# Row normalisation: loads and stores on two DMA queues, whole 8 MB tiles, rows split between VectorE and ScalarE

## The chip, the cores and the metric

The kernel runs on one core of a Trainium2 chip. The metric is the device time of one execution in microseconds (us), lower is better. Unless a sentence says otherwise, a time is the median of all timed runs of a kernel, and a ratio is the mean time of one kernel's fast runs over the mean time of the other's fast runs of the same rounds. So a ratio is not quite the ratio of the medians that are quoted.

"Span" is the profiled length.

## The reference

```python
def reference(x):                      # x: float32 [32, 512, 1024]
    sums = np.sum(np.abs(x), axis=-1, keepdims=True)
    return (x / (sums + 1e-8)).astype(np.float32)
```

There are 16,384 rows of 1,024 numbers. Every row is read once (67.11 MB in all), divided by the sum of its absolute values, and written once (67.11 MB).

## The kernel before

A tile is 128 partitions by 16 rows, 8 MB, so that each partition reads and writes 64 KB in one contiguous piece. There are eight tiles and three buffers. All transfers, loads and stores, go to one hardware queue, which is issued by SyncE. VectorE sums all 16 rows of a tile in one instruction and scales ten of them; ScalarE scales six. The last two tiles are handled in four chunks of four rows, and each chunk is stored as soon as it is ready.

```python
    def process_chunk(x_tile, out_ap, r0, rN, mv):
        ...
        nc.vector.tensor_reduce(out=s, in_=x_tile[:, r0 : r0 + rN, :], axis=X, op=add,
                                apply_absolute_value=True)
        nc.vector.reciprocal(out=inv, in_=s)
        for r in range(rN):
            if r < mv:  nc.vector.tensor_scalar_mul(...)      # row r of the chunk
            else:       nc.scalar.activation(..., func=Copy, scale=inv[:, r : r + 1])
        nc.sync.dma_start(out=out_ap[:, r0 : r0 + rN, :], in_=x_tile[:, r0 : r0 + rN, :])

    for i in range(ntiles):                                   # ntiles = 8, R = 16, MV = 10
        x_tile = sbuf.tile([P, R, d], x.dtype)                # BUFS = 3
        nc.sync.dma_start(out=x_tile[:, :, :], in_=x_t[i, :, :, :])
        if i < ntiles - 2:
            process_chunk(x_tile, out_t[i], 0, R, MV)
        else:
            C = 4
            for c0 in range(0, R, C):
                process_chunk(x_tile, out_t[i], c0, C, (MV * C) // R)
```

(Cut and shortened.) A scheduler orders these instructions. On the one queue it makes three loads, three stores, three loads, three stores, two loads, and then the eight chunk stores.

## Time and profile before

The time is 318.40 us (318.33 to 318.67, five runs). The next lines are from the page of the profiled execution: the span; the mean busy share of the 16 DMA engines in 40 slices of the span, in tenths; the DMA queue with its packets, MB and share of the 16 engines' time; the chain of waits by engine; and the three costliest groups (line, engine, operation, shapes, count | busy us, mean ns of one | idle time before them and its releaser).

```profile
span 316.9 us, 261 instructions
...
DMA  9999999999999999999999999999999999999797
...
q1 hardware_dynamic: 3168, 134.22, 98.6%
...
DVE 57%; DMA 35%; issue 4%; ACT 0%; ACTq 0%; SPq 0%; DVEq 0%
...
L37 DVE TENSOR_REDUCE s<-x_tile 128x4 f32<-128x4096 f32 (+1 forms) x14 | 138.3, 9891 | 111.2 <-DMA x_tile<-in_x_dram 111.2
L54 ACT ACTIVATE x_tile<-x_tile,inv 128x1024 f32<-128x1024 f32 x52 | 55.4, 1137 | 223.9 <-DVE inv L45 223.9
L48 DVE TENSOR_SCALAR x_tile<-x_tile,inv 128x1024 f32<-128x1024 f32 x76 | 51.4, 748 | 0.3
```

The queue line is the one that counts: one queue keeps 16 engines busy for 98.6% of the span. The chain of waits gives VectorE 57%, but that is the share of one dependency path. While VectorE works on a tile, the queue moves others. VectorE itself waits 111.2 us for loads.

In the records of single DMA packets, a packet of 64 KB takes 2.418 us at the median, and 16 engines x 65,536 B / 2.418 us is 433.7 GB/s. The Trainium skill, "DMA: Bandwidth & Descriptors", section "Where 436 GB/s comes from", puts the ceiling of the 16 ports at 435.2 GB/s; the trace agrees within 0.4%. One tile is 8 such packets on each engine, 19.35 us, and eight loads and eight stores are 309.5 us. A change can win only by taking idle time away from the DMA engines. For each kernel two numbers are therefore worked out from the packet records:

- *busy*: the summed durations of the data packets, divided by 16;
- *idle*: from the first data packet to the last, the time in which engines had no data packet, as a mean over the 16.

For the kernel before, busy is 312.3 us and idle is 2.1 us. The other 2.5 us of the span are before the first packet and after the last, less about 0.6 us in which two packets overlap on an engine and are counted twice.

### The profile page before, as it was taken

Reading aid. Unit: us, or ns where it says so; the run is one execution under the profiler, and the core shown is the slowest. Engines: PE = TensorE matmul, PEld = TensorE weight load, DVE = VectorE, ACT = ScalarE, POOL = GpSimd, SP = SyncE. Lnnn points to the kernel's source line nnn. Section 1 sums busy time; section 2 is a strip of 40 time slices with the busy share of each in tenths; the row PEclk is TensorE's granted clock in tenths of the full one; section 3 lists DMA queues with packets and bytes.
Section 4 is the critical chain, followed back from the end, with each engine's and each line's share of the span. In section 5 each row is a group of like instructions: output and inputs, shape, how many; then the busy total and the mean of one; then the engine's idle time right before and its main releaser. Section 6 shows DMA issues by size and latency. Waiting matters only on the chain.

```text
span 316.9 us, 261 instructions
## 1 busy us (share of the span) xinstructions
DVE 190.8 (60%) x104; ACT 56.7 (18%) x53; POOL 0.2 (0%) x4
## 2 busy tenths in 40 slices
DVE  0019999999990000039999999980000069999910
ACT  0010080080080000000160070080000002522520
POOL 0000000000000000000000000000000000000000
DMA  9999999999999999999999999999999999999797
GB/s 397 397 397 513 414 397 397 397 438 488 397 397 505 422 397 397 521 405 397 480 447 397 397 489 438 397 430 480 414 397 480 438 405 422 399 431 432 335 430 331
DMA packets 3170, 134.24 MB, mean 424 GB/s; under 512 B 352, under 2 KB 352, under 8 KB 352
## 3 DMA queue, kind: packets, MB, share of 16 engines
q1 hardware_dynamic: 3168, 134.22, 98.6%
q14 instruction: 2, 0.02, 0.0%
HBM read 67.11 MB, written 67.11 MB: 424 GB/s over the span
## 4 chain that ended last, share of the span: by engine, by line
DVE 57%; DMA 35%; issue 4%; ACT 0%; ACTq 0%; SPq 0%; DVEq 0%
DVE s L37 41%; DMA x_tile<-in_x_dram 35%; DVE x_tile L48 15%; DVE inv L45 1%; ACT x_tile L54 0%; ACTq L99 0%; SPq L60 0%; DVEq L45 0%; DVEq L48 0%
## 5 line engine op out<-in xcount | busy, mean ns | idle before, releaser
L37 DVE TENSOR_REDUCE s<-x_tile 128x4 f32<-128x4096 f32 (+1 forms) x14 | 138.3, 9891 | 111.2 <-DMA x_tile<-in_x_dram 111.2
L54 ACT ACTIVATE x_tile<-x_tile,inv 128x1024 f32<-128x1024 f32 x52 | 55.4, 1137 | 223.9 <-DVE inv L45 223.9
L48 DVE TENSOR_SCALAR x_tile<-x_tile,inv 128x1024 f32<-128x1024 f32 x76 | 51.4, 748 | 0.3
L54 ACT ACT_TABLE_LOAD x1 | 1.3, 1283 | 22.8 <-DMA x_tile<-in_x_dram 22.8
L45 DVE RECIPROCAL inv<-s 128x4 f32<-128x4 f32 (+1 forms) x14 | 2.6, 200 | 0.4
L88 POOL MEMSET const-bfloat16-1.0<- 128x1 bf16 x1 | 0.1, 101 | 0.0
L88 POOL MEMSET const-uint8-127<- 128x1 uint8 x1 | 0.1, 101 | 0.0
L88 POOL MEMSET const-float32-0.0<- 128x1 f32 x1 | 0.1, 98 | 0.2 <-issue 0.2
L88 POOL MEMSET const-float32-1.0<- 128x1 f32 x1 | 0.1, 98 | 0.0
## 6 DMA issues: line engine op xcount, KB each, us to landing
out_dram<-x_tile SPq DMA_DIRECT2D x8, 2048.0 KB, 9.9
x_tile<-in_x_dram SPq DMA_DIRECT2D x8, 51.0
out_dram<-x_tile SPq DMA_DIRECT2D x6, 29.5
```

The costliest lines, as they stand in the source:

```text
L37: nc.vector.tensor_reduce(out=s[:, :], in_=x_tile[:, r0 : r0 + rN, :], axis=mybir.AxisListType.X, op=mybir.AluOpType.add, apply_absolute_v ...
L45: nc.vector.reciprocal(out=inv[:, :], in_=s[:, :])
L48: nc.vector.tensor_scalar_mul(out=x_tile[:, r0 + r, :], in0=x_tile[:, r0 + r, :], scalar1=inv[:, r : r + 1],)
L54: nc.scalar.activation(out=x_tile[:, r0 + r, :], in_=x_tile[:, r0 + r, :], func=mybir.ActivationFunctionType.Copy, scale=inv[:, r : r + 1],)
L88: nc = _bacc.Bacc("TRN2", target_bir_lowering=False, num_devices=1)
```

## The change

The intent: two queues, so that stores do not line up behind loads; VectorE relieved by giving ScalarE seven rows to sum (absolute value with an accumulated sum, the result itself dropped into PSUM) and to scale; and simple whole-tile stores. Instructions stay in program order.

```diff
-    for i in range(ntiles):
-        x_tile = sbuf.tile([P, R, d], x.dtype)
-        nc.sync.dma_start(out=x_tile[:, :, :], in_=x_t[i, :, :, :])
-        if i < ntiles - 2:
-            process_chunk(x_tile, out_t[i], 0, R, MV)
-        else:
-            ...                                  # four chunks, four stores
+    DVE_PARTS = [(0, 5), (5, 9)]
+    ACT_PARTS = [(9, 13), (13, 16)]
+
+    def compute(x_tile):
+        sums = []
+        for a, b in ACT_PARTS:
+            s = stats.tile([P, b - a], FP32)
+            for r in range(a, b):
+                junk = psum.tile([P, d], FP32)
+                nc.scalar.activation(out=junk[:, :], in_=x_tile[:, r, :],
+                                     func=ACTF.Abs, accum_out=s[:, r - a : r - a + 1])
+            sums.append(s)
+        for k, (a, b) in enumerate(DVE_PARTS):
+            ...                                  # VectorE: reduce rows a..b, add EPS, reciprocal, scale
+            a2, b2 = ACT_PARTS[k]
+            inv2 = inverse(sums[k], b2 - a2)     # VectorE: add EPS, reciprocal
+            for r in range(a2, b2):
+                ...                              # ScalarE: scale row r by inv2 (Copy)
+
+    with tc.manual_schedule():
+        for i in range(ntiles):
+            x_tile = sbuf.tile([P, R, d], FP32)
+            nc.sync.dma_start(out=x_tile[:, :, :], in_=x_t[i])
+            compute(x_tile)
+            nc.gpsimd.dma_start(out=out_t[i], in_=x_tile[:, :, :])
```

(Shortened.) Below, tiles are counted from one: the last tile is the eighth, and "the seventh store" is the store of the seventh tile.

More of the change, by code (lines that the diff above doesn't have):

```diff
@@ L7 @@
 from concourse._compat import with_exitstack
+FP32 = mybir.dt.float32
+EPS = 1e-8
 @with_exitstack
@@ L18 @@
     P = nc.NUM_PARTITIONS
+    ACTF = mybir.ActivationFunctionType
     x_flat = x.flatten_outer_dims()
@@ L26 @@
     ntiles = n // (P * R)
+    BUFS = 3
     x_t = x_flat.rearrange("(n p r) d -> n p r d", p=P, r=R)
     out_t = out_flat.rearrange("(n p r) d -> n p r d", p=P, r=R)
-    BUFS = 3
     sbuf = ctx.enter_context(tc.tile_pool(name="sbuf", bufs=BUFS))
-    stats = ctx.enter_context(tc.tile_pool(name="stats", bufs=BUFS))
-    def process_chunk(x_tile, out_ap, r0, rN, mv):
-        s = stats.tile([P, rN], mybir.dt.float32, tag="s")
-        nc.vector.tensor_reduce(
-            out=s[:, :],
-            in_=x_tile[:, r0 : r0 + rN, :],
-            axis=mybir.AxisListType.X,
-            op=mybir.AluOpType.add,
-            apply_absolute_value=True,
-        )
-        inv = stats.tile([P, rN], mybir.dt.float32, tag="inv")
-        nc.vector.reciprocal(out=inv[:, :], in_=s[:, :])
-        for r in range(rN):
-            if r < mv:
+    stats = ctx.enter_context(tc.tile_pool(name="stats", bufs=6))
@@ new lines, with inverse @@
+    psum = ctx.enter_context(
+        tc.tile_pool(name="psum", bufs=2, space=bass.MemoryType.PSUM)
+    )
+    def inverse(s, k):
+        nc.vector.tensor_scalar_add(out=s[:, :], in0=s[:, :], scalar1=EPS)
+        inv = stats.tile([P, k], FP32)
+        nc.vector.reciprocal(out=inv[:, :], in_=s[:, :])
+        return inv
+    DVE_PARTS = [(0, 5), (5, 9)]
[6 more added lines that the diff above has]
+                junk = psum.tile([P, d], FP32)
+                nc.scalar.activation(
+                    out=junk[:, :],
+                    in_=x_tile[:, r, :],
+                    func=ACTF.Abs,
+                    accum_out=s[:, r - a : r - a + 1],
+                )
+            sums.append(s)
+        for k, (a, b) in enumerate(DVE_PARTS):
+            s = stats.tile([P, b - a], FP32)
+            nc.vector.tensor_reduce(
+                out=s[:, :],
+                in_=x_tile[:, a:b, :],
+                axis=mybir.AxisListType.X,
+                op=mybir.AluOpType.add,
+                apply_absolute_value=True,
+            )
+            inv = inverse(s, b - a)
+            for r in range(a, b):
+                row = x_tile[:, r, :]
@@ L48, in process_chunk @@
                 nc.vector.tensor_scalar_mul(
-                    out=x_tile[:, r0 + r, :],
-                    in0=x_tile[:, r0 + r, :],
-                    scalar1=inv[:, r : r + 1],
-                )
-            else:
+                    out=row, in0=row, scalar1=inv[:, r - a : r - a + 1]
+                )
+            a2, b2 = ACT_PARTS[k]
+            inv2 = inverse(sums[k], b2 - a2)
+            for r in range(a2, b2):
+                row = x_tile[:, r, :]
                 nc.scalar.activation(
-                    out=x_tile[:, r0 + r, :],
-                    in_=x_tile[:, r0 + r, :],
-                    func=mybir.ActivationFunctionType.Copy,
-                    scale=inv[:, r : r + 1],
-                )
@@ L60, in process_chunk @@
-        nc.sync.dma_start(out=out_ap[:, r0 : r0 + rN, :], in_=x_tile[:, r0 : r0 + rN, :])
-    MV = 10
-    for i in range(ntiles):
-        x_tile = sbuf.tile([P, R, d], x.dtype)
-        nc.sync.dma_start(out=x_tile[:, :, :], in_=x_t[i, :, :, :])
-        if i < ntiles - 2:
-            process_chunk(x_tile, out_t[i], 0, R, MV)
-        else:
-            C = 4
-            for c0 in range(0, R, C):
-                process_chunk(x_tile, out_t[i], c0, C, (MV * C) // R)
+                    out=row,
@@ L77 @@
+                    in_=row,
+                    func=ACTF.Copy,
+                    scale=inv2[:, r - a2 : r - a2 + 1],
+                )
+    with tc.manual_schedule():
[4 more added lines that the diff above has]
+            nc.gpsimd.dma_start(out=out_t[i], in_=x_tile[:, :, :])
 _INS = ['x']
```

## The prediction

> **What bounds the kernel now.** The DMA engines. Section 3 of the page: the one hardware queue takes 98.6% of the time of 16 engines, for 134.22 MB; section 2 shows DMA at nine tenths in nearly every slice. In the DMA records a 64 KB packet takes 2.418 us at the median, loads and stores alike: 16 x 65,536 B / 2.418 us = 433.7 GB/s. The Trainium skill, "DMA: Bandwidth & Descriptors", section "Where 436 GB/s comes from", gives 435.2 GB/s as the ceiling of the 16 ports; the trace agrees within 0.4%. One 8 MB tile is 8 packets per engine, 19.35 us; 16 tile transfers are 309.5 us of the 316.9 us span. The other 7 us are 2.7 before the first packet, 0.7 in slow first packets, small losses, and about 2 at the end. The chain of waits names VectorE for 57%; that misleads: while VectorE works, the queue moves other tiles.
>
> **What the change does.**
> - VectorE per tile falls from 17.2 (reduce of 16 rows) + 0.25 + 6.7 (ten scales) = 24.2 us to about 5.4 + 4.4 (reduces of 5 and 4 rows at 1.076 us) + 6.1 (nine scales at 0.67) + 1.2 for eight tiny instructions = 17 us.
> - ScalarE gets seven Abs passes with an accumulated sum (estimate 1.06 us each as the Copy has, plus 0.2 for the accumulator: 8.8 us) beside seven Copies (7.4 us). Its last three Copies wait for VectorE's last reciprocal, so a tile takes about 20.4 us from landing to store, against 24.2.
> - Neither is on the critical path in the middle: a tile's load and store take 38.7 us of DMA.
> - Loads and stores share the 16 engines from two queues; the bytes stay. A packet should look about twice as long while both are active, the total staying at about 430 GB/s.
> - The last two tiles are no longer stored in pieces. The last tile's compute (20.4 us, plus about 1.5 of software issue) hides behind the seventh store (19.35 us), except that the last load ends behind the sixth store (estimate 2 to 3 us, it was issued that much later). I expect 2 to 6 us of idle DMA there.
>
> The Trainium skill, "SBUF — State Buffer", section "SBUF: two separate sides", says that VectorE in a two-port mode locks GpSimd out of writing descriptors. The scales seem to run so (1024 elements in 0.67 us), but each of the eight stores is issued as VectorE starts a reduce; no run here shows it yet. I expect under 2 us.
>
> **Sum.** Head 2.7 + 0.7, transfers 309.5, gap 4, receipt and end 2: span about 319, and the timed runs read 1.45 us more: **320.0 us**, 0.5% slower, range 315.5 to 328. Chances: faster by over 2% 0.05, within 2% 0.75, slower by over 2% 0.20.
>
> **What the profile would show.** DMA queues together 96 to 98% of 16 engines' span, half each; VectorE busy about 136 us, ScalarE about 130; VectorE's idle time larger, released by load DMAs; the last store landing 20 to 21 us after its issue with nothing else moving, and a dip in DMA before it.
>
> **What would make it wrong.** Slower: packets of the software queue costing more than 2.418 us (smaller descriptors, ring fetches, writes and reads alternating): 3% on all would be 9 us; a late start of each software store; arbitration that makes the last tile late. Faster: two queues letting an engine overlap reads and writes beyond 434 GB/s, which nothing in the trace suggests.

## The result, and the profile after

The time is 326.98 us (325.81 to 329.18, five runs) against 318.40; the ratio is 1.0282, 95% interval 1.0252 to 1.0311. The change is 2.8% slower. Its runs also differ by 3.4 us, where those of the kernel before differ by 0.3.

The same lines of the page, for the changed kernel:

```profile
span 327.4 us, 415 instructions
...
DVE 137.3 (42%) x152; ACT 120.2 (37%) x169; POOL 4.6 (1%) x12
...
DMA  9899899899899998998999999999899998960695
...
q1 hardware_dynamic: 1152, 67.11, 48.0%
q0 software_dynamic: 1152, 67.11, 47.4%
...
L66 DVE TENSOR_REDUCE s<-x_tile 128x5 f32<-128x5120 f32 (+1 forms) x16 | 79.0, 4939 | 161.7 <-DMA x_tile<-in_x_dram 161.7
L57 ACT ACTIVATE junk<-x_tile 128x1024 f32<-128x1024 f32 x56 | 56.5, 1008 | 138.2 <-DMA x_tile<-in_x_dram 138.2
L83 ACT ACTIVATE x_tile<-x_tile,inv 128x1024 f32<-128x1024 f32 x56 | 59.9, 1137 | 45.6 <-DVE inv L44 45.6
```

VectorE went from 190.8 to 137.3 us and waits longer for loads, so it is not the limit. The queues together fell from 98.6% to 95.4% of the span, and the DMA row shows where: a hole in the 37th slice, near the end. The view of windows for the changed kernel gives it numbers (stretch in us: its length, busy time of VectorE, ScalarE and GpSimd with instruction counts, TensorE clock, DMA share, GB/s):

```profile
0.00:255.00 255.00, 114.56 (x125) 99.86 (x143) 3.53 (x10) 1.00 1.00 429
255.00:285.00 30.00, 6.50 (x10) 6.37 (x7) 0.53 (x1) 1.00 1.00 433
285.00:293.00 8.00, 7.90 (x8) 6.45 (x14) 0.00 (x0) 1.00 0.91 393
293.00:306.00 13.00, 8.32 (x12) 7.49 (x7) 0.53 (x1) 1.00 0.05 20
306.00:328.00 22.00, 0.00 (x0) 0.00 (x0) 0.00 (x0) 1.00 0.88 381
```

The kernel before, same view, has no such stretch:

```profile
0.00:255.00 255.00, 144.76 (x72) 39.37 (x37) 0.20 (x4) 1.00 1.00 429
255.00:285.00 30.00, 28.40 (x18) 8.64 (x8) 0.00 (x0) 1.00 0.98 421
285.00:300.00 15.00, 15.00 (x11) 6.45 (x6) 0.00 (x0) 1.00 0.92 394
```

Up to 255 us both kernels move 429 GB/s. From 293 to 306 us the changed kernel moves almost nothing. In the packet records its busy time is 312.0 us (312.3 before) and its idle time 12.3 us (2.1 before). The idle time alone accounts for 10.2 us of the 10.5 us by which the spans differ. (This profile is of the slowest of the five runs, 329.18 us; the medians differ by 8.6 us.)

The timeline shows what the DMA engines wait for. These lines are the start of the last tile's first reduction on VectorE, released by the load, and the last store's issue on GpSimd, released by ScalarE's last scale (start us, us taken, instruction [idle before <- releaser]):

```profile
284.06 5.49 DVE L66 TENSOR_REDUCE s<-x_tile 128x5 f32<-128x5120 f32 x1 [23.36 <-DMA x_tile<-in_x_dram]
...
305.05 0.53 POOL L95 DMA_DIRECT2D out_dram<-x_tile  x1 [40.26 <-ACT x_tile L83]
```

The last tile lands at 284.06 us, is computed for 21.0 us, and its store is issued at 305.05 us. Its first packet starts about 1.1 us later. On the typical engine the seventh store's data ended at 293.7 us, so there is nothing left to move for 12.4 us.

### The profile page after: what moved, and what is told of

It is laid out like the page before. It is cut to its first block, busy times and chain, and to the rows that moved or that the text cites. A ratio compares the mean times of both kernels' runs of the same rounds, so it can differ in the third digit from the quotient of the medians.

```text
span 327.4 us, 415 instructions
## 1 busy us (share of the span) xinstructions
DVE 137.3 (42%) x152; ACT 120.2 (37%) x169; POOL 4.6 (1%) x12
## 4 chain that ended last, share of the span: by engine, by line
another core or an unknown queue 51%; DMA 27%; DVE 10%; ACT 3%; issue 1%; SPq 1%; POOLq 0%
DMA x_tile<-in_x_dram 27%; DVE s L66 6%; DVE x_tile L76 4%; ACT junk L57 2%; ACT x_tile L83 1%; SPq L93 1%; DVE inv L44 0%; DVE s L42 0%; POOLq L121 0%; POOLq L95 0%
## 5 line engine op out<-in xcount | busy, mean ns | idle before, releaser
L66 DVE TENSOR_REDUCE s<-x_tile 128x5 f32<-128x5120 f32 (+1 forms) x16 | 79.0, 4939 | 161.7 <-DMA x_tile<-in_x_dram 161.7
L57 ACT ACTIVATE junk<-x_tile 128x1024 f32<-128x1024 f32 x56 | 56.5, 1008 | 138.2 <-DMA x_tile<-in_x_dram 138.2
L83 ACT ACTIVATE x_tile<-x_tile,inv 128x1024 f32<-128x1024 f32 x56 | 59.9, 1137 | 45.6 <-DVE inv L44 45.6
L76 DVE TENSOR_SCALAR x_tile<-x_tile,inv 128x1024 f32<-128x1024 f32 x72 | 49.2, 749 | 0.8 <-DVE inv L44 0.3
L57 ACT ACTIVATION_READ_ACCUMULATOR junk<-x_tile 128x1 f32 x56 | 10.5, 187 | 0.0
L95 POOL DMA_DIRECT2D out_dram<-x_tile x8 | 4.4, 548 | 300.7 <-ACT x_tile L83 300.7
L44 DVE RECIPROCAL inv<-s 128x4 f32<-128x4 f32 (+2 forms) x32 | 5.8, 181 | 1.1
L42 DVE TENSOR_SCALAR s<-s 128x4 f32<-128x4 f32 (+2 forms) x32 | 5.3, 167 | 0.5
```

The source lines that it names most:

```text
L42: nc.vector.tensor_scalar_add(out=s[:, :], in0=s[:, :], scalar1=EPS)
L44: nc.vector.reciprocal(out=inv[:, :], in_=s[:, :])
L57: nc.scalar.activation(out=junk[:, :], in_=x_tile[:, r, :], func=ACTF.Abs, accum_out=s[:, r - a : r - a + 1],)
L66: nc.vector.tensor_reduce(out=s[:, :], in_=x_tile[:, a:b, :], axis=mybir.AxisListType.X, op=mybir.AluOpType.add, apply_absolute_value=True,)
L76: nc.vector.tensor_scalar_mul(out=row, in0=row, scalar1=inv[:, r - a : r - a + 1])
L83: nc.scalar.activation(out=row, in_=row, func=ACTF.Copy, scale=inv2[:, r - a2 : r - a2 + 1],)
```

## The experiments

Theory A says: the loss is idle DMA time at the end, because a tile that is not divided cannot start to leave before all of it is computed. Rival B says: stores from the software queue, or two queues side by side, cost time throughout. A second question, theory C, came from the packet records: in the changed kernel the last load ended on most engines at 274 to 275 us, but on three engines only at up to 281 us. Are the two queues the reason for the late landing?

### One: the last tile alone stored in pieces (a1_pieces)

```diff
+            if i == ntiles - 1: compute(x_tile, out_t[i])   # after each of the four parts:
+                # nc.gpsimd.dma_start(out=out_ap[:, a:b, :], in_=x_tile[:, a:b, :])
+            else:
                 compute(x_tile)
                 nc.gpsimd.dma_start(out=out_t[i], in_=x_tile[:, :, :])
```

> The changed kernel with the last tile alone stored in four pieces (5, 4, 4 and 3 rows), each as soon as it is scaled. Theory A (the whole loss is DMA idle after the seventh store, while the undivided last tile is computed): the 12 us of idle engines before the last store shrink to 0 to 2 us, span 315 to 317, time 317 to 319. Rival B (stores through the software queue, or two queues side by side, cost time all along): time stays at 324 or more.

The time was 318.62 us, ratio to before 1.0004 (0.9990 to 1.0019). Busy was 312.7, idle 1.2 us. The whole loss was gone with two queues, the software queue and the new compute all still in place. Theory A holds and rival B, a cost throughout, falls. The timeline of GpSimd shows the four issues of the last tile, the first of them 9.7 us after the landing at 281.58 us:

```profile
291.24 0.53 POOL L80 DMA_DIRECT2D out_dram<-x_tile  x1 [26.78 <-DVE inv L44]
295.82 1.04 POOL L92 DMA_DIRECT2D out_dram<-x_tile  x1 [4.06 <-ACT x_tile L85]
299.02 0.53 POOL L80 DMA_DIRECT2D out_dram<-x_tile  x1 [2.16 <-DVE inv L44]
302.57 0.53 POOL L92 DMA_DIRECT2D out_dram<-x_tile  x1 [3.01 <-ACT x_tile L85]
```

### Two: the second queue a hardware queue (a2_act_queue)

```diff
-            nc.gpsimd.dma_start(out=out_t[i], in_=x_tile[:, :, :])
+            nc.scalar.dma_start(out=out_t[i], in_=x_tile[:, :, :])
```

> The changed kernel with its whole-tile stores issued by ScalarE, so from a second hardware queue. Theory A: the gap stays, since the last tile's compute stays, time 324 to 329 if engines drift apart between any two queues, about 320 to 321 if the drift of three engines (about 7 of the 12 us of gap) belongs to the software queue. Rival B in its form 'software descriptors cost time': back to 318 to 319, with no gap.

325.90 us, ratio 1.0235 (1.0204 to 1.0266); idle 8.9 us. Without any software queue nearly all of the loss stayed. Late engines showed here too: the last load's data ended at 274.3 us on the median engine and at 277.8 us on the last.

### Three: the kernel before, with whole last tiles (a3_one_queue_whole)

```diff
-        if i < ntiles - 2:
+        if i < ntiles:
             process_chunk(x_tile, out_t[i], 0, R, MV)
```

> The kernel before with one edit: the last two tiles are computed and stored whole. Theory A: VectorE does both tiles in 2 x 24.2 us after the landing at 256.6, so the last store starts near 306.5, with about 10 us of idle DMA in two gaps; span about 327, time 328. Rival B: nothing but small change, 318 to 320.

328.44 us, ratio 1.0312 (1.0294 to 1.0329); busy 312.1, idle 12.5 us in two gaps, 7.3 us before the seventh store and 4.8 us before the eighth. This one edit costs the old kernel as much as the whole change does. VectorE's 24.2 us for each of the two tiles are exposed one after the other.

### Four: the kernel before, with the software queue for its stores (a4_before_sw_queue)

```diff
-        nc.sync.dma_start(out=out_ap[:, r0 : r0 + rN, :], in_=...)
+        nc.gpsimd.dma_start(out=out_ap[:, r0 : r0 + rN, :], in_=...)
```

> The kernel before with one edit: stores issued from GpSimd (software queue), the last two tiles still in pieces, its own compute. Theory A: packets of the software queue still 2.418 us; a first piece of the last tile comes about 14.5 us after landing, so a gap of 0 (no drift) to 6 us (drift of the last load by 7 us as in the changed kernel): time 317 to 322. Rival B: 326 or more.

320.73 us, ratio 1.0071 (1.0054 to 1.0088); busy 312.6, idle 4.0 us. Software-queue packets of 64 KB took 2.418 us at the median, as those of the hardware queue did. So the queue pair costs this kernel about 2 us, again as idle time near the end, and not through slower packets.

### Five: no compute in the last tile (b1_last_uncomputed)

```diff
-            compute(x_tile)
+            if i < ntiles - 1:
+                compute(x_tile)
```

> The changed kernel with no compute at all in the last tile (a wrong result on purpose: the last eighth is stored as loaded). Theory A: landing to store falls from 21 us to about 1, the last store is queued while the seventh still runs, the idle time before it falls from 12 us to under 0.5, and the time to 316.5 to 318. Rival (the gap is something of the last software store itself, not of the compute): a gap of several us stays, time 321 or more.

The result was wrong. 318.20 us (317.15 to 319.57), ratio 1.0000 (0.9967 to 1.0034); idle 1.3 us. The last store was issued at 280.23 us, as soon as the tile had landed, and no gap before it remained. The median came out slightly above the 316.5 to 318 expected, and the runs scatter by 2.4 us. In the profile, of a run of 317.49 us, the engines ended 1.3 us apart; what the slower runs lost was not looked into. The gap itself is the last tile's compute.

### Six: the changed kernel's compute and whole tiles, on one queue (c1_one_queue_split)

```diff
-        for i in range(ntiles):
-            x_tile = sbuf.tile([P, R, d], FP32)
-            nc.sync.dma_start(out=x_tile[:, :, :], in_=x_t[i])
-            compute(x_tile)
-            nc.gpsimd.dma_start(out=out_t[i], in_=x_tile[:, :, :])
+        for g in range(0, ntiles, BUFS):
+            group = range(g, min(g + BUFS, ntiles))
+            tiles = []
+            for i in group:
+                x_tile = sbuf.tile([P, R, d], FP32)
+                nc.sync.dma_start(out=x_tile[:, :, :], in_=x_t[i])
+                tiles.append(x_tile)
+            for i, x_tile in zip(group, tiles):
+                compute(x_tile)
+                nc.sync.dma_start(out=out_t[i], in_=x_tile[:, :, :])
```

> The changed kernel's compute and whole tiles, but all transfers from the one hardware queue, in groups of three loads and three stores as in the kernel before. Theory C (of the 12 us of gap about 7 come from three engines that fell behind with the last load because two queues share them): in one queue all engines finish the last load near 276.5; idle about 3.3 us before the seventh store and 1 to 2 before the last, span 320 to 321.5, time 321.5 to 323. Rival (the queues do not matter, only the undivided tile): time 326 to 328.

319.96 us, ratio 1.0055 (1.0040 to 1.0070); idle 4.3 us, of which 3.8 us lie before the seventh store and none before the eighth. That is better than expected, and 7 us better than the changed kernel with the same compute and the same undivided tiles. The last tile landed at 275.97 us instead of 284.06. Its landing is in the timeline:

```profile
275.97 5.49 DVE L66 TENSOR_REDUCE s<-x_tile 128x5 f32<-128x5120 f32 x1 [1.90 <-DMA x_tile<-in_x_dram]
```

(In a second profile of the changed kernel, the eleventh experiment, it landed at 280.40 us.) So how the transfers are queued does matter, through the time at which the last load lands. But the order on the one queue differs too (both last loads go ahead of the seventh store), and this run does not separate that from the number of queues.

Why the load lands late is seen in the view of DMA, cut to the short stretch in which it ends. For the changed kernel from 276 to 278 us, then from 278.2 to 284 us (packets, bytes; then per queue: packets, MB, share of the engines' time):

```profile
DMA packets 29, 1.05 MB, mean 524 GB/s; under 512 B 13, under 2 KB 13, under 8 KB 13
...
q0 software_dynamic: 15, 0.98, 113.4%
q1 hardware_dynamic: 14, 0.07, 7.9%
```

```profile
DMA packets 45, 2.75 MB, mean 475 GB/s; under 512 B 3, under 2 KB 3, under 8 KB 3
...
q0 software_dynamic: 41, 2.69, 106.8%
q1 hardware_dynamic: 4, 0.07, 2.6%
```

The packets below 512 B are 4-byte completion writes, one for each engine and transfer. In the first stretch the load's queue (q1) has one data packet and 13 of them; in the second it has one data packet and the last 3. So 13 engines were done 276.7 us into the run (their median), and VectorE waited until 284.06 us for the other three. On one queue the same stretch is short and complete, all 16 completion writes between 272 and 276.5 us:

```profile
DMA packets 22, 0.39 MB, mean 87 GB/s; under 512 B 16, under 2 KB 16, under 8 KB 16
...
q1 hardware_dynamic: 22, 0.39, 20.4%
```

The records do not name an engine, but packets of one engine follow each other end to start, so that the order on each engine can be pieced together. One of the 13, in the changed kernel (L, S: a 64 KB packet of a load or store; l, s: a completion write):

```
LLLLLLLLlLLLLLLLLlLLLSLSLSLSLSLSlSSsSSLSLSLSLSLSLSLsLSlSLSLSLSLSLSLSLsLSlSL...
```

With both queues filled, the engine takes one packet of each in turn (two of one queue in succession are rare in the records), and **a completion write of four bytes takes a turn like any other packet**: after the load's last data packet comes a 64 KB packet of the store, and only then the load's completion. For the changed kernel's last load the data ended at 274.4 us on the median engine and the completion was written at 276.8; for the last engine the two were 281.3 and 283.7 us. That is one packet, 2.4 us, in both. In the one-queue kernel the completion follows the data at once. The Trainium skill, "DMA: Bandwidth & Descriptors", section "Queues, rings and completion order", says that an engine goes round its queues packet by packet, with about 9 to 17 descriptors to a packet. The turns are in the trace, but here a turn is a single 64 KB packet or a single completion write.

### Seven and eight: the size of a packet (b2_parts_8_8 and b3_parts_8_8_16k)

The control takes parts of four rows everywhere; the second run also pads the tile by 64 bytes after each four rows, so that a packet is 16 KB.

```diff
-    DVE_PARTS = [(0, 5), (5, 9)]
-    ACT_PARTS = [(9, 13), (13, 16)]
+    DVE_PARTS = [(0, 4), (4, 8)]
+    ACT_PARTS = [(8, 12), (12, 16)]
# and in the second run only:
-            x_tile = sbuf.tile([P, R, d], FP32)
+            x_tile = sbuf.tile([P, 4, 4 * d + 16], FP32)    # 4 rows, 64 B of padding; loads and stores accordingly
```

> Control for the next run: the changed kernel with 8 rows for VectorE and 8 for ScalarE, in parts of 4, packets of 64 KB as before. The last tile's compute becomes about 20.1 us in place of 21.0: time 325 to 328, last load's last packets spread over 4 to 8 us across engines, 9 to 12 us of idle DMA.

> As the control, but the tile is padded by 64 bytes after each 4 rows, so that every packet is 16 KB instead of 64 KB. A 16 KB packet took 0.611 us, so busy time rises by 1% (about 3 us). Theory C in the form that engines fall behind by whole packets: spread of the last load 1 to 2.5 us, idle DMA 5 to 8 us, time 322 to 325. Rival (the spread comes from slow packets and not from their size): spread and idle as in the control, time 328 to 331.

The control took 324.27 us (ratio 1.0179, 1.0156 to 1.0202, so unclear against the 2% line), idle 8.1 us, both a little below what was expected. The padded one took 326.51 us (ratio 1.0260), busy 314.5 and idle 8.0 us. Neither rival got it right. Small packets did what theory C said of them: the last engine ended the last load 0.8 us after the median one (3.2 us in the control), and its completion came 0.6 us after its data (2.4 us). But the load's data ended later on *all* engines, at 279.7 us at the median against 274.5, and so the tile landed at 281.41 us against 280.46, and no idle time was saved.

Why it ended later can be counted in the order of the packets. From this load's first packet to its last, every engine of the control ran 8 packets of the load and only 6 of the store, all of 64 KB, in 33.8 us; in the padded run most engines ran 32 and 30, all of 16 KB, in 37.6 us (medians). So against an even share the store missed two packets in both: one turn went to a completion write of its queue, and the load, which began this stretch, also ended it. Two missed packets of 64 KB save the load more time than two of 16 KB. The other 1.3 us are a later first packet (242.0 us against 240.7). No run changed the turns by themselves. What the pair does show is that straggling engines are one way for a load to land late, and an evenly shared load is another.

### Nine: the best parts together (d1_one_queue_split_pieces)

One queue as in the sixth run, and the last two tiles stored in four pieces each, as in the first run, by the same queue.

```diff
+                if i >= ntiles - 2:
+                    compute(x_tile, out_t[i])              # four pieces
+                else:
                     compute(x_tile)
                     nc.sync.dma_start(out=out_t[i], in_=x_tile[:, :, :])
```

> Candidate for a better kernel: the split compute of the changed kernel, all transfers on the one hardware queue in groups of three loads and three stores, and the last two tiles stored in four pieces each. The engines' busy time of about 312 us stays; idle time should fall from 2.1 us before to under 0.7: span 315 to 316, time 316.5 to 317.7, 0.3 to 0.6% faster than before. If something other than idle time holds the kernel before, no gain.

318.01 us against 318.13 in the same rounds, ratio 0.9995 (0.9983 to 1.0008): the same. The expectation failed. Busy 312.2 and idle 2.0 us: no gap before any store was left, but 1.8 us of idle time lay in the last microseconds, where the engines ended up to 2 us apart. The kernel before ended all 16 within 0.2 us. No version here beats the kernel before by a measurable amount; there were only 2.1 us of idle time to win.

### Ten: the old compute with the two other parts of the change (a5_before_sw_queue_whole)

The kernel before with the edits of the third and the fourth run together.

```diff
-        nc.sync.dma_start(out=out_ap[:, r0 : r0 + rN, :], in_=...)
+        nc.gpsimd.dma_start(out=out_ap[:, r0 : r0 + rN, :], in_=...)
-        if i < ntiles - 2:
+        if i < ntiles:
```

> The kernel before with two edits: stores from the software queue and whole last tiles, its own compute. By the sum that fits the changed kernel (idle = how far the last load lands behind a full seventh store, 6 to 10 us, plus compute, here 24.3 us, plus 1.5 us to issue and start, less 19.35 us of store) the idle time is 13 to 17 us, span 328 to 332, time 329.5 to 333.5. A rival in which the split of rows cost time would have this run at or below the changed kernel's 327.

329.84 us, ratio 1.0384 (1.0351 to 1.0417); idle 12.0 us, a little under the expected 13 to 17 because the last load landed at 279.60 us. VectorE and ScalarE took 24.9 us from there to the store's issue, where the changed kernel took 21.0. So the split of rows shortens an exposed tile by 3.9 us; by the medians it is worth 2.9 us (329.84 against 326.98).

### Eleven: the changed kernel once more (r1_changed_again)

> The changed kernel again, for a second profile. The executions differ by up to 3.4 us; if that is the straggling of a few engines in the last load, then this profile's span less the first one's 327.4 equals the difference of the two landing times of the last tile (284.06 in the first) within 0.5 us, with compute and last store unchanged.

This is a single run, 325.53 us. Its span was 323.8 us, 3.6 us shorter than that of the first profile, and its last tile landed at 280.40 us, 3.66 us earlier; the compute was again 21.0 us:

```profile
280.40 5.49 DVE L66 TENSOR_REDUCE s<-x_tile 128x5 f32<-128x5120 f32 x1 [21.35 <-DMA x_tile<-in_x_dram]
...
301.39 0.53 POOL L95 DMA_DIRECT2D out_dram<-x_tile  x1 [38.26 <-ACT x_tile L83]
```

So the difference between these two executions is the time at which the last load landed. In this one the last engine ended the load's data 1.4 us behind the median engine, in the first profile 6.9 us.

### All of it in one table

Spans, busy and idle times are of the profiled execution, in us; the time is the median of all runs.

| kernel | queues | last tile(s) | compute | time | span | busy | idle |
|---|---|---|---|---|---|---|---|
| before | one | pieces | old | 318.40 | 316.9 | 312.3 | 2.1 |
| changed | two, software | whole | split | 326.98 | 327.4 | 312.0 | 12.3 |
| a1 | two, software | last in pieces | split | 318.62 | 316.7 | 312.7 | 1.2 |
| a2 | two, hardware | whole | split | 325.90 | 322.9 | 311.5 | 8.9 |
| a3 | one | whole | old | 328.44 | 327.1 | 312.1 | 12.5 |
| a4 | two, software | pieces | old | 320.73 | 319.5 | 312.6 | 4.0 |
| a5 | two, software | whole | old | 329.84 | 326.8 | 311.8 | 12.0 |
| c1 | one | whole | split | 319.96 | 318.3 | 311.5 | 4.3 |
| d1 | one | pieces | split | 318.01 | 316.6 | 312.2 | 2.0 |
| b1 | two, software | whole, not computed | split | 318.20 | 315.7 | 311.5 | 1.3 |
| b2 | two, software | whole | split, 8 and 8 rows | 324.27 | 323.1 | 312.0 | 8.1 |
| b3 | two, software, 16 KB packets | whole | split, 8 and 8 rows | 326.51 | 324.4 | 314.5 | 8.0 |

In all kernels of the table but b3, loads go in packets of 64 KB and busy time lies between 311.5 and 312.7 us. Neither the queues nor the compute changes it. The idle time is what differs.

## Why the prediction was right or wrong

**What bounds the kernel: right.** The busy time of the DMA engines stayed at 312 us through every variant. The part of it that placed the first packet at 2.7 us was off by 1 us: the DMA view shows it at 1.7 us, and what was missing there lies at the end.

**The compute: about right.** VectorE was to be busy about 136 us and was 137.3; ScalarE about 130, and was 120.2, because an absolute-value pass and its accumulator read overlap (seven of them took 7.4 us, not 8.8). A tile was to take 20.4 us from landing to store plus 1.5 us to start it; it took 21.0 plus 1.1. The queues together were to take 96 to 98% of the span and took 95.4%.

**The software queue as such: right.** Its packets cost no more than those of the hardware queue, and replacing it by a hardware queue kept the loss (325.90 us). The Trainium skill, "SBUF — State Buffer", section "SBUF: two separate sides", says that while VectorE runs in a two-port mode, GpSimd is locked out and cannot write descriptors. All eight issues of the changed kernel took 0.53 us on GpSimd, but for the first, 0.67 us. Three issues that fell among VectorE's row scales took longer: 1.04 us in the first experiment, 0.89 and 0.90 us in the fourth, and each ended 0.12 us after the end of a scale that had begun within 0.2 us of the issue. Two others in the fourth, also issued during scales, took 0.53 us. So up to half a microsecond may be the lock, which no run tested by itself; the forecast of under 2 us in all holds.

**Packets twice as long while both queues are active: wrong.** Each still took 2.418 us. An engine runs one packet at a time and alternates, so the sharing shows as a longer time from issue to landing, not as longer packets.

**The step that failed: the landing of the last load.** The prediction put it so: the compute "hides behind the seventh store (19.35 us), except that the last load ends behind the sixth store (estimate 2 to 3 us, it was issued that much later)", and it expected "2 to 6 us of idle DMA there". The place and the form of the sum were right, but this term was mis-sized, and its reason, the later issue, left out what made it large. The prediction did list "arbitration that makes the last tile late" among its risks, but put no number on it. With the seventh store's data ending at 293.7 us, a full store of 19.35 us would have begun at 274.35. The last load landed at 284.06, so the lag was 9.7 us, not 2 to 3. The sum then closes: 9.7 + 21.0 + 1.1 - 19.35 = 12.45 us, and the gap was 12.4. Of the 9.7 us, nothing was lost on the median engine's data (274.4 us); 6.9 us were the last of three engines that had fallen behind (281.3); 2.4 us were the completion write waiting for its turn behind a store packet (283.7); 0.4 us passed until VectorE started. In the other profiles of two-queue kernels with whole tiles and large packets the lag, worked out in the same way, was 5.2 to 6.4 us. In the second profile of the changed kernel it was 5.2 us: about 1.1 on the median engine's data, 1.4 for the last engine, 2.4 for the completion write and 0.4 to the start. The first profile was of the slowest of the five runs, 2.2 us above the median. So the turn of the completion write is there in each, and the straggling engines are what varies most.

**Wrong class, inside the range.** 326.98 us lies within 315.5 to 328, but only 1 us from its end: the central 320.0 was 7 us too low, and "within 2%" had been given 0.75. That the range held is owed to its width and not to the sum. The trace of before could not show the wait of the completion write, because with one queue it follows the data at once.

**What stays open.** Three engines had packets that were a few tenths of a microsecond too long in the changed kernel, again and again. Up to the end of the last load, all packets of these engines together took 4.0 to 6.5 us more than 2.418 us each, those of the others 1.5 to 2.2 us. The worst of them began the last load 5.2 us behind the median engine, so most of its delay was older than that load. Why it was those packets and those engines was not found. The account of turns is read from the order of packets; no run controlled the turns themselves.

## What to carry to other kernels

Where the DMA engines are busy 98% of the time, judge a change by the idle time that it gives them, above all between the last load and the last store: that tile's compute and its latencies are hidden only by transfers that are still waiting, so let the last tile leave in pieces. When loads and stores share the engines from two queues, do not estimate when a load lands from bandwidth alone: it lands when the slowest engine has written its completion, and that write waits its turn behind a full packet of the other queue (2.4 us here). An undivided tile on one queue can be cheap (1.6 us here, with the quicker compute and both last loads ahead of the last two stores), so ask of each part of a change separately what it adds.

## What the Trainium skill lacked or had wrong

- "DMA: Bandwidth & Descriptors", section "Queues, rings and completion order", describes turns at packet granularity, but not that a completion write takes such a turn. With 64 KB packets it came 2.4 us after the last data while the other queue was filled, with 16 KB packets 0.6 us, and at once on a single queue. The section's typical 9 to 17 descriptors to a packet were not seen: turns alternated after one piece of 64 KB or of 16 KB.
- The same page, section "Issuing engines are not separate DMA queues", says that issuing from several engines concurrently only saves the sequencer's time. The bandwidth agrees (busy 312.0 us with two queues, 312.3 with one), but a cost is missing: the last load landed at 284.06 and 280.40 us in two profiles with two queues, at 275.97 us with one queue, where the order of the last transfers differed as well. Moving only the stores to a second queue cost the kernel before 2.2 us (318.50 to 320.73, fourth experiment).
- No page has a figure for how far the engines drift apart when two queues share them: the last engine ended the last load's data 1.3 to 6.9 us behind the median one with 64 KB packets, and 0.8 us with 16 KB.
- The same page, section "Anatomy of one DMA", gives a fixed cost of about 2.0 us to a DMA on the software queue. Here the last store, which ran alone, took 21.0 us from issue to landing, about 1.65 us more than its 19.35 us of packets; 1.1 us of that came before the first packet. So the page's figure is a little high for this transfer.
